# One inference step of a hybrid decoder layer: other PSUM bank counts, new states on two tags, and a group norm four quarter-units later

## The chip, the cores and the metric

The kernel runs on one core of one Trainium2 chip. The time is that of the whole program on the device, in microseconds (us). Before the change three runs took 1208.07, 1210.54 and 1215.57 us; their median is 1210.54 us.

## The reference

One layer of a decoder with two branches. There are 272 prompt rows (16 learned meta tokens and 256 prompt tokens) and 64 sample rows (8 sequences of 8 new tokens, which continue from carried states). All in float32.

```python
xn = rms_norm(h, norm_w)
proj = xn @ w_in                       # 2048 -> z_ssd, xBC, dt, z_pool, u, two gates
xbc_act, conv_new = causal_dwconv(xbc, conv_hist, conv_w, conv_b)      # 4 taps, silu
dt = softplus(dt_raw + dt_bias);  a = -exp(a_log)
y, state = ssd_segment(...)            # per chunk: y_diag + y_off, h = h * decay + B^T xdt
y = (y + xs * d_skip) * silu(z_ssd)
yg = y.reshape(..., 4, 512)            # gated norm over each of the 4 groups
yg = yg * rsqrt(mean(yg * yg) + EPS)
branch_ssd = (yg * ssd_norm_w) @ w_proj_ssd
mixed = einsum(pooled, pool_mix_w) + pool_mix_b    # pooled: causal means less u, per group
branch_pool = (mixed * pool_scale * silu(z_pool)) @ w_proj_pool
h_new = h + (gate_ssd * branch_ssd + gate_pool * branch_pool) @ w_out
y_out = rms_norm(h_new, final_norm_w)
```

The new states of the sample sequences (32 heads x 64 x 128 for each of 8) are outputs too.

## The kernel before

**Units and quarters.** The weights are cut into 156 units (UNITS, line 50), in this order: B 0 to 3, C 4 to 7, xs 8 to 23, z 24 to 39, then the SSD gate (gs) and the branch product (br), the pool stage (u, zp, mix), the pool gate (gp), its product (bp), and the output (wo, and wx at the end). A unit gives 128 output columns for all rows. Its 16 chunks of K are multiplied three times each (high weights with high operand, high with low, low with high; lines 235 to 237, half_k), 48 matmuls into one PSUM accumulator. A quarter-unit is 12 of them. Quarter q of unit i has the number 4i + q.

**Order.** Everything is laid out by hand (manual_schedule): each engine runs its instructions in the order in which the program issues them. The main loop (line 869) goes through the quarters. Before a quarter's matmuls it issues, for a half-unit three halves ahead, the high part of the weights on ACT (line 147, in even quarters), and after it the low part on DVE (line 153, in odd quarters); the load of a raw half on SP's queue (line 136) follows the low part that frees its buffer. After a quarter's matmuls tick(q) issues what was put down for that quarter with at(q, f) or later(d, f); later(1, f) is the next quarter's tick. A function that stands in a tick earlier than another was put down earlier.

**PSUM.** Eight banks go to three tags of the pool `ps`: "acc" for accumulators (NACC, line 32), "tr" for transposes, state-space outputs and some accumulators (NTR), and "st" (two, the pool's default) for sums, spreads, state products. A new tile of a tag takes the bank of an older one and its first writer waits for that one's last reader, on whichever engine it is.

**The state-space stage.** ssd_stages_of(g) puts the stages of group g down from tick 52 + 24g on (SSD_AT, SSD_STEP), so groups 0 to 3 begin at 52, 76, 100 and 124. The plan (line 622) holds offsets. Those that matter here: s_yoff1 at 8 and 10 (an "st" tile each, copied by ACT a tick later), s_dec(2) and s_dec(3) at 10 and 12 (differences on DVE, a tick later exponentials on ACT at lines 518 to 522, another later the products with cb on DVE at lines 528 and 530), s_y(2) and s_y(3) at 15 and 17 (line 560, "tr"; they read those products), s_new(q) at 17, 19, 21, 23, s_yoff2 at 20 and 21 (line 585, "tr"; read on DVE at lines 594 to 596), and s_pstate at 25 ("st"). s_new(q) is what gives pair q of the sample sequences its new state: two matmuls (line 613, "st") for sequences 2q and 2q + 1, each added to the decayed old state by DVE one tick later (line 615). The old states are decayed on POOL (line 605).

**The gated norm.** z_evac (line 639), one tick after a z unit, multiplies by rstd (line 637), a tick later takes silu on ACT (645), then multiplies into y on DVE (646), and three ticks after the evacuation squares on ACT: the first unit of a group into the tile gn[g] (line 649; tag "ss", one buffer), the others into a tile that POOL adds to gn[g] (line 654). norm_group(g) sits at tick 4 x (unit of z 4g + 3) + 9, that is 117, 133, 149 and 165. It calls spread_rstd (line 160): matmuls with gn[g] as the stationary operand into an "st" tile (line 165), one tick later scale and square root (lines 170 and 171), two later the reciprocal with a Newton step and three diagonal matrices on DVE (174 to 179), three later matmuls that spread the result over the partitions into another "st" tile (184), four later the products with y on DVE (661). y_split(g) (line 665) cuts y into a high and a low part for the br units and sits at ticks 170 to 173; br 0 is unit 44 (quarters 176 to 179, and its last quarter reads group 3).

Of the kernel before, what the change touches and what calls it, by code (L numbers as in the profile page):

```python
# [6 lines left out]
F32 = mybir.dt.float32  # L7
# [21 lines left out]
CBW = 480  # L29
CB2 = 400  # L30
NU0 = 8
NACC, NTR, NWARM = 3, 3, 16
SSD_AT, SSD_STEP = 52, 24
NWXS = 6
CHUNK = ((0, 128), (128, 128), (256, 64))
# [33 lines left out]
def hybrid_step(tc, ctx, io):  # L69
# [7 lines left out]
    ps = ctx.enter_context(tc.tile_pool(name="ps", bufs=2, space=PSUM))  # L77
# [6 lines left out]
    def slot(name, shape, dt=F32):  # L84
        tag = free_slots.pop(0)
        t = pool_of(tag).tile(shape, dt, tag=tag, name=name)
        live[name] = tag
        return t
# [6 lines left out]
    def drop(*names):  # L95
        for n in names:
            free_slots.append(live.pop(n))
# [14 lines left out]
    def pc(name, i):  # L112
        o, _ = _PC[name]
        return par[:, o + i:o + i + 1]
# [4 lines left out]
    def at(q, f):  # L119
        assert q >= now[0]  # L120
        sched.setdefault(q, []).append(f)

    def later(d, f):
        at(now[0] + d, f)
# [19 lines left out]
    def prep_hi(i, h):  # L144
        r = raws[i, h]
        hi = slot(f"wxh{i}_{h}", [128, HW], F32R) if kept(i, h) else wp.tile([128, HW], F32R, tag="hi", name=f"hi{i}_{h}")
        S.activation(hi, r, AF.Copy)  # L147
        whl[i, h] = hi
# [11 lines left out]
    def spread_rstd(ss, n, scale, name, done):  # L160

        at_ = (0, 128, n - 128)
        p = ps.tile([128, 512], F32, tag="st", name=f"ps_sum{name}")
        for i, t0 in enumerate(at_):
            PE.matmul(p[:, i:i + 1], lhsT=ss[:, t0:t0 + 128], rhs=ones[:, 0:1], start=True, stop=True, skip_group_check=True)
        v, t, r = (tp.tile([128, 3], F32, tag=f"f{j}", name=f"sr{name}{j}", bufs=1) for j in range(3))
        dg = tp.tile([128, 3, 128], F32, tag="dg", name=f"dg{name}", bufs=1)

        def f1():
            V.tensor_scalar(out=v, in0=p[:, 0:3], scalar1=scale, scalar2=EPS, op0=ALU.mult, op1=ALU.add)  # L170
            S.activation(t, v, AF.Sqrt)

        def f2():
            V.reciprocal(out=r, in_=t)
            V.tensor_tensor(out=t, in0=r, in1=r, op=ALU.mult)
            V.scalar_tensor_tensor(out=t, in0=t, scalar=-0.5, in1=v, op0=ALU.mult, op1=ALU.mult)
            V.scalar_tensor_tensor(out=r, in0=t, scalar=1.5, in1=r, op0=ALU.add, op1=ALU.mult)
            for i in range(3):
                V.tensor_scalar(out=dg[:, i, :], in0=ident, scalar1=r[:, i:i + 1], scalar2=None, op0=ALU.mult)

        def f3():
            q = ps.tile([128, 512], F32, tag="st", name=f"ps_rs{name}")
            for i, t0 in enumerate(at_):
                PE.matmul(q[:, t0:t0 + 128], lhsT=ones, rhs=dg[:, i, :], start=True, stop=True, skip_group_check=True)
            later(1, lambda: done(q))
        later(1, f1)
        later(2, f2)
        later(3, f3)
# [225 lines left out]
    def ssd_stages_of(g):  # L414
        sd = ssd["p"]
        Bg, Cg = Bs[:, g, :], Cs[:, g, :]
        st = {}
# [189 lines left out]
        def s_new(q):  # L607
            def f():
                for b in (2 * q, 2 * q + 1):
                    p = ps.tile([128, 512], F32, tag="st", name=f"ps_hn{g}_{b}")  # L610
                    j = b % 4
                    r = st["R"][32 * j:32 * j + 3 * DEC, b // 4, :].bitcast(F32R)
                    PE.matmul(p, lhsT=r[:, 512:XB], rhs=r[:, 0:512], start=True, stop=True, tile_position=(32 * j, 0))  # L613
                    h = st["hin", q][:, b % 2, :]
                    later(1, lambda h=h, p=p: V.tensor_tensor(out=h, in0=h, in1=p, op=ALU.add))
            return f
# [40 lines left out]
    def norm_group(g):  # L657
        def scale(r):
            for c in range(4):
                y = xs[g][:, c, NMETA:T]  # L660
                V.scalar_tensor_tensor(out=y, in0=y, scalar=pc("ssd_norm_w", 4 * g + c), in1=r[:, :TV], op0=ALU.mult,
                                       op1=ALU.mult)
        spread_rstd(gn[g], TV, 1.0 / 512, f"g{g}", scale)

    def y_split(g):
        h = slot(f"yh{g}", [128, 4, TV], F32R)
        l = slot(f"yl{g}", [128, 4, TV], F32R)
        y = xs[g][:, :, NMETA:T]
        S.activation(h, y, AF.Copy)
        yh.append(h)  # L670
        yl.append(l)

        def low():
            V.tensor_tensor(out=l, in0=y, in1=h.bitcast(F32), op=ALU.subtract)
            drop(f"xs{g}")
        later(1, low)
# [116 lines left out]
    def both_parts(q):  # L793
        for e, t in enumerate((mh, ml)):
            S.activation(fin["hl"][:, 4 * q:4 * q + 4, e, :], t[q][:, :, 256:TV].bitcast(F32), AF.Copy)
# [50 lines left out]
    first = {}  # L846
    for i, (kind, idx) in enumerate(UNITS):
        first.setdefault((kind, idx), i)
    for g in range(G):
        at(4 * first["z", 4 * g + 3] + 9, lambda g=g: norm_group(g))  # L850

    tscope = ExitStack()

    def late():
        scope.close()
        extra["p"] = ctx.enter_context(tc.tile_pool(name="slots2", bufs=1))
        free_slots.extend(f"x{j}" for j in range(10))
        extra["t"] = tscope.enter_context(tc.tile_pool(name="tp2", bufs=2))
        drop("Bs", "Cs")
        SY.dma_start(out=io["opold"], in_=io["spold"])  # L860
        for g in range(4):
            at(4 * first["gs", 0] + 10 + g, lambda g=g: y_split(g))

    prep(*halves[6])
# [4 lines left out]
    for i, (kind, idx) in enumerate(UNITS[:NU - 4]):  # L869
        if i < 2:  # L870
            at(14 + 2 * i, lambda i=i, k=kind, j=idx: evac(i, k, j, acc2[i]))
            continue
        if i == NU0:
            start.close()
            ssd["p"] = scope.enter_context(tc.tile_pool(name="ssd", bufs=1))
            for g in range(G):
                for d, f in ssd_stages_of(g):
                    at(SSD_AT + SSD_STEP * g + d, f)
        if (kind, idx) == ("gs", 0):
            late()  # L880
        if (kind, idx) == ("u", 0):
            drop(*[n for q in range(4) for n in (f"yh{q}", f"yl{q}")])
        if (kind, idx) == ("bp", 0):
            drop(*[n for q in range(4) for n in (f"xh{q}", f"xl{q}")])
        if (kind, idx) == ("wo", 0):
            drop(*[n for q in range(4) for n in (f"ph{q}", f"pl{q}")])
            for q in range(3):
                hn[q] = slot(f"hn{q}", [128, 4, TV])
                SY.dma_start(out=hn[q], in_=io["xT"][:, 4 * q:4 * q + 4, NMETA:T])
            tscope.close()  # L890
            extra["f"] = ctx.enter_context(tc.tile_pool(name="fin", bufs=1))
            fin["xy"] = extra["f"].tile([128, 2, 512], F32, name="xres")
            fin["xw"] = slot("xrw", [128, 2, 512])
            fin["hl"] = extra["f"].tile([128, KT, 2, 64], F32R, name="hl")
            SY.dma_start(out=fin["xy"], in_=io["xres"][0:256, :].rearrange("(c p) f -> p c f", c=2))
            SY.dma_start(out=fin["xw"][0:64, 0, :], in_=io["xres"][256:320, :])
            SY.dma_start(out=fin["xw"][:, 1, :], in_=io["fwb"])
            for q in range(4):
                at(4 * i + 2 + 4 * q, lambda q=q: both_parts(q))
        if kind == "mix":  # L900
            acc = [ps.tile([128, 512], F32, tag="tr" if c < 3 else "acc", name=f"acc{i}_{c}", bufs=3) for c in range(4)]
        else:
            acc = ps.tile([128, 512], F32, tag="tr" if i == 3 else "acc", name=f"acc{i}", bufs=NACC)
        for qq in range(4):
            if qq % 2 == 0:
                n = place.get(2 * i + qq // 2 + 3, len(halves) - 1)
                for x in halves[done:n + 1]:
                    prep_hi(*x)
            else:
                for x in halves[done:n + 1]:  # L910
                    prep_lo(*x)
                done = n + 1
                load_to(n + 5)
            quarter_mm(i, qq, acc, kind, idx)
            if kind == "mix":
                at(4 * i + qq + 1, lambda g=idx, c=qq, a=acc: mix_evac(g, c, a[c]))
            elif qq == 3:
                at(max(4 * i + 4, 14 + 2 * i), lambda i=i, k=kind, j=idx, a=acc: evac(i, k, j, a))
            tick(4 * i + qq)
# [56 lines left out]
    for j, (t0, n) in enumerate(CHUNK):  # L976
        acc = ps.tile([128, 512], F32, tag="acc", name=f"accx{j}", bufs=NACC)
# [115 lines left out]
```

## Time and profile before

| | |
|---|---|
| median of three runs | 1210.54 us |
| profiled execution, its own time | 1208.65 us |
| its span, first to last instruction | 1206.7 us |
| mean granted TensorE clock | 0.998 |
| PE, PEld busy | 1191.6, 1152.8 us |
| DVE, ACT, POOL busy | 731.7, 531.9, 84.1 us |

PE is TensorE's matmuls and PEld its weight loads, DVE is VectorE, ACT ScalarE, POOL GpSimd, and SP the queue that issues transfers. A row of the timeline gives the start in us from the span's start, the length in us, the engine, the line, the operation, output<-input by the program's names, the shapes, how many instructions are merged in it, and in brackets how long the engine stood idle before it and what ended that. In a merged row matmuls overlap, and a matmul's length has its way through the array in it, so the next one starts earlier than the row ends. A row of the windows gives the stretch, its length, then for PE, PEld, DVE, ACT and POOL the busy time and the number of instructions, the granted clock as a share of full speed, the mean busy share of the transfer engines and GB/s.

### The profile page before, as it was taken

The numbers are of one execution on the slowest core, as the hardware profiler recorded it, in microseconds if no ns is written. First come the engines' busy times: TensorE is split into PE (matmuls) and PEld (weight loads), VectorE is DVE, ScalarE is ACT, GpSimd is POOL, SyncE is SP. The second block draws the span as 40 slices with busy tenths as digits, with TensorE's granted clock in tenths as the row PEclk, the third lists the DMA queues.
The fourth block names the chain that finished last, engine by engine and source line by source line (L and its number), as shares of the span: only waits on it lengthen the run. The fifth ranks groups of instructions, "written<-read, shape, count | busy, mean of one in ns | idle before, by whom it ended". The sixth has DMA issues, their size and how long they took to land.

```text
span 1206.7 us, 19815 instructions
## 1 busy us (share of the span) xinstructions
PE 1191.6 (99%) x8015; PEld 1152.8 (96%) x8015; DVE 731.7 (61%) x1138; ACT 531.9 (44%) x728; POOL 84.1 (7%) x82
## 2 busy tenths in 40 slices
PE   9999999999999999999999999999999999999996
PEld 7999889898989999999999999999999999999995
DVE  7786898898875644444457474765454455555634
ACT  6555636383835433333333433434343333335531
POOL 0000141433231000000000000000000000000000
PEclk9999999999999999999999999999999999999999
DMA  7645667676764444444456454544444444446612
GB/s 282 198 150 168 215 214 241 215 256 215 228 209 156 148 149 155 142 157 144 154 162 179 152 158 159 157 153 156 145 152 154 144 156 147 151 176 230 227 40 88
DMA packets 86087, 207.66 MB, mean 172 GB/s; under 512 B 26876, under 2 KB 32092, under 8 KB 85980
## 3 DMA queue, kind: packets, MB, share of 16 engines
q1 hardware_dynamic: 85836, 205.36, 51.4%
q8 instruction: 63, 1.03, 0.4%
q0 software_dynamic: 160, 1.03, 0.3%
q14 instruction: 28, 0.23, 0.1%
HBM read 189.05 MB, written 17.77 MB: 171 GB/s over the span
## 4 chain that ended last, share of the span: by engine, by line
PE 92%; DVE 4%; DMA 2%; issue 1%; ACT 1%; SPq 0%; DVEq 0%; ACTq 0%
PE acc L235 28%; PE acc L236 28%; PE acc L237 28%; PE accx L985 2%; DVE cacc L342 1%; PE acc L280 1%; DVE lo L153 1%; DMA bc<-acT 1%; PE ps_y L560 1%; PE ps_st L545 1%; PE ps_hn L613 1%; DMA raw<-wall 0%; DVE M L513 0%; DVE M L528 0%; PE ps_yo L572 0%
## 5 line engine op out<-in xcount | busy, mean ns | idle before, releaser
L147 ACT ACTIVATE hi<-raw 128x1024 fp32r<-128x1024 f32 x306 | 323.8, 1059 | 548.4 <-PE acc L236 387.9
L153 DVE TENSOR_TENSOR lo<-raw,hi 128x1024 fp32r<-128x1024 f32 x306 | 380.2, 1243 | 246.6 <-ACT hi L147 246.5
L235 PE MATMUL acc<-xh,hi 128*128 128x320 f32 (+4 forms) x1632 | 511.8, 314 | 0.0
L236 PE MATMUL acc<-xl,hi 128*128 128x320 f32 (+4 forms) x1632 | 507.7, 311 | 0.0
L237 PE MATMUL acc<-xh,lo 128*128 128x320 f32 (+4 forms) x1632 | 506.7, 310 | 0.0
L235 PEld LDWEIGHTS acc<-xh,hi 128*128 128x128 f32 x1632 | 306.6, 188 | 6.3 <-issue 4.0
L237 PEld LDWEIGHTS acc<-xh,lo 128*128 128x128 f32 x1632 | 306.9, 188 | 0.0
L236 PEld LDWEIGHTS acc<-xl,hi 128*128 128x128 f32 x1632 | 306.7, 188 | 0.0
L236 PE MATMUL acc<-yl,hi 128*128 128x320 f32 x256 | 79.0, 309 | 0.0
L235 PE MATMUL acc<-yh,hi 128*128 128x320 f32 x256 | 79.0, 308 | 0.0
L237 PE MATMUL acc<-yh,lo 128*128 128x320 f32 x256 | 78.9, 308 | 0.0
L237 PE MATMUL acc<-ph,lo 128*128 128x320 f32 x256 | 78.9, 308 | 0.0
L236 PE MATMUL acc<-pl,hi 128*128 128x320 f32 x256 | 78.8, 308 | 0.0
L235 PE MATMUL acc<-ph,hi 128*128 128x320 f32 x256 | 78.7, 308 | 0.0
L237 PE MATMUL acc<-mh,lo 128*128 128x320 f32 x192 | 59.3, 309 | 0.0
L235 PE MATMUL acc<-mh,hi 128*128 128x320 f32 x192 | 59.3, 309 | 0.0
L236 PE MATMUL acc<-ml,hi 128*128 128x320 f32 x192 | 59.3, 309 | 0.0
L605 POOL TENSOR_TENSOR hin<-hin,E 128x512 f32<-128x512 f32 x32 | 49.5, 1575 | 49.2 <-ACT E L522 32.9
L342 DVE SCALAR_TENSOR_TENSOR cacc<-rawf,par,cacc 128x360 f32<-128x360 f32 (+1 forms) x72 | 50.7, 705 | 1.8
L237 PEld LDWEIGHTS acc<-ph,lo 128*128 128x128 f32 x256 | 48.1, 188 | 0.0
L236 PEld LDWEIGHTS acc<-pl,hi 128*128 128x128 f32 x256 | 48.1, 188 | 0.0
L235 PEld LDWEIGHTS acc<-ph,hi 128*128 128x128 f32 x256 | 48.0, 188 | 0.0
(237 smaller groups left out, 1194.3 us busy)
## 6 DMA issues: line engine op xcount, KB each, us to landing
raw<-wall SPq DMA_DIRECT2D x312, 512.0 KB
hin<-ssmT SPq DMA_DIRECT2D x16, 512.0 KB
ossms<-hin SPq DMA_DIRECT2D x16, 512.0 KB
bc<-acT SPq DMA_DIRECT2D x8, 672.0 KB
x<-xT SPq DMA_DIRECT2D x3, 672.0 KB
R<-tail SPq DMA_DIRECT2D x32, 60.0 KB
hn<-xT SPq DMA_DIRECT2D x3, 640.0 KB
opool<-u SPq DMA_DIRECT2D x16, 100.0 KB
```

The costliest lines, as they stand in the source:

```text
L147: S.activation(hi, r, AF.Copy)
L153: V.tensor_tensor(out=lo, in0=r, in1=hi.bitcast(F32), op=ALU.subtract)
L235: PE.matmul(acc[:, :n], lhsT=hi[:, c], rhs=bh, start=first, stop=False)
L236: PE.matmul(acc[:, :n], lhsT=hi[:, c], rhs=bl, start=False, stop=False)
L237: PE.matmul(acc[:, :n], lhsT=lo[:, c], rhs=bh, start=False, stop=last)
L280: PE.matmul(acc2[u][:, :T], lhsT=w[part // 2][:, cc], rhs=(wl if part == 1 else wh)[q][:, c, :], start=(k == 0 and part == 0), stop=(k == ...
L342: V.scalar_tensor_tensor(out=a[:, a0:], in0=r[:, a0 + k:k + ACCW], scalar=pc("conv_w", 4 * c + k), in1=a[:, a0:], op0=ALU.mult, op1=ALU.add)
L545: PE.matmul(p, lhsT=st["bt"][:, i, :], rhs=st["xdt"][:, i, :], start=(i == 0), stop=False)
L560: PE.matmul(p[64 * e:64 * e + 64, a:b], lhsT=st["xdt"][:n, i, 64 * hh:64 * hh + 64], rhs=m[:n, e, o:o + b - a], start=(i == 0), stop=(i == ...
L605: GP.tensor_tensor(out=hv, in0=hv, in1=E, op=ALU.mult)
L613: PE.matmul(p, lhsT=r[:, 512:XB], rhs=r[:, 0:512], start=True, stop=True, tile_position=(32 * j, 0))
L985: PE.matmul(acc, lhsT=st, rhs=wx(part, k), start=(k == 0 and o == 0), stop=(k == KT - 1 and part == 1))
```

## The change

"acc" goes from three banks to two and "tr" from three to four ("st" keeps two). Unit 2 joins unit 3 in "tr", and the four accumulators of a mix unit all take "tr". Of the new states, pairs 0 and 2 stay in "st" and pairs 1 and 3 go to "tr". norm_group goes from +9 to +13, to ticks 121, 137, 153 and 169. The last y_split no longer has a tick of its own but follows one tick after the products of its group's norm, at 174 and not 173.

```diff
-NACC, NTR, NWARM = 3, 3, 16
+NACC, NTR, NWARM = 2, 4, 16
...
         def s_new(q):
             def f():
                 for b in (2 * q, 2 * q + 1):
-                    p = ps.tile([128, 512], F32, tag="st", name=f"ps_hn{g}_{b}")
+                    p = ps.tile([128, 512], F32, tag=("st", "tr")[q % 2], name=f"ps_hn{g}_{b}", bufs=(2, NTR)[q % 2])
...
                 V.scalar_tensor_tensor(out=y, in0=y, scalar=pc("ssd_norm_w", 4 * g + c), in1=r[:, :TV], op0=ALU.mult,
                                        op1=ALU.mult)
+            if g == 3:
+                later(1, lambda: y_split(g))
         spread_rstd(gn[g], TV, 1.0 / 512, f"g{g}", scale)
...
     for g in range(G):
-        at(4 * first["z", 4 * g + 3] + 9, lambda g=g: norm_group(g))
+        at(4 * first["z", 4 * g + 3] + 13, lambda g=g: norm_group(g))
...
         SY.dma_start(out=io["opold"], in_=io["spold"])
-        for g in range(4):
+        for g in range(3):
             at(4 * first["gs", 0] + 10 + g, lambda g=g: y_split(g))
...
         if kind == "mix":
-            acc = [ps.tile([128, 512], F32, tag="tr" if c < 3 else "acc", name=f"acc{i}_{c}", bufs=3) for c in range(4)]
+            acc = [ps.tile([128, 512], F32, tag="tr", name=f"acc{i}_{c}", bufs=NTR) for c in range(4)]
         else:
-            acc = ps.tile([128, 512], F32, tag="tr" if i == 3 else "acc", name=f"acc{i}", bufs=NACC)
+            acc = ps.tile([128, 512], F32, tag="tr" if i in (2, 3) else "acc", name=f"acc{i}",
+                          bufs=NTR if i in (2, 3) else NACC)
```

## The prediction

> **What bounds the kernel now.** I read the page first.
>
> ```profile
> span 1206.7 us, 19815 instructions
> PE 1191.6 (99%) x8015; PEld 1152.8 (96%) x8015; DVE 731.7 (61%) x1138; ACT 531.9 (44%) x728; POOL 84.1 (7%) x82
> ```
>
> PE is busy for 99% of the span, so time can only be won or lost where PE stands still. Next, the busy time by stretches, a steady one and one in the state-space stage:
>
> ```profile
> 450.00:600.00 150.00, 150.00 (x1026) 150.00 (x1025) 63.04 (x64) 48.66 (x52) 0.00 (x0) 1.00 0.44 151
> 150.00:170.00 20.00, 18.40 (x124) 16.22 (x121) 19.66 (x29) 7.93 (x15) 14.38 (x13) 1.00 0.61 187
> ```
>
> In the steady stretch 1026 matmuls take 150 us, 146.2 ns each, so a quarter-unit (12 matmuls) is 1.755 us, which I call a quarter. In the second stretch PE loses 1.6 us while DVE is full (19.66 of 20). PE's timeline shows where: at the matmuls for the new states, line 613. The rows below hold a wait in state-space group 0, one in group 1, the undisturbed form, and (two rows) one in group 2.
>
> ```profile
> 161.52 1.09 PE L613 MATMUL ps_hn<-R 24*128 24x512 f32 x2 [1.50 <-DVE hin L615]
> 221.54 1.09 PE L613 MATMUL ps_hn<-R 24*128 24x512 f32 x2 [0.24 <-DVE hin L615]
> 279.54 0.50 PE L613 MATMUL ps_hn<-R 24*128 24x512 f32 x2
> 285.52 0.50 PE L613 MATMUL ps_hn<-R 24*128 24x512 f32 x1
> 287.02 0.46 PE L613 MATMUL ps_hn<-R 24*128 24x512 f32 x1 [1.00 <-PE ps_hn L613]
> ```
>
> Undisturbed, a pair runs side by side in 0.50. At 161.52 it waits 1.50 for the additions that free its banks and then runs one after the other (1.09 - 0.50 = 0.59): 2.09. At 221.54: 0.24 + 0.59 = 0.83. At 285.52 the second of the pair comes 1.46 late. That one's releaser is on DVE:
>
> ```profile
> 285.00 1.92 DVE L661 SCALAR_TENSOR_TENSOR xs<-xs,par,ps_rsg 128x320 f32<-128x320 f32 x4
> ```
>
> It ends at 286.92, and PE goes on 0.10 later. The bank was held by the spread rstd of norm group 0, which these four products read. So a matmul can wait for a reader that stands later in the program. In all 2.09 + 0.83 + 1.46 = 4.38 us.
>
> **The change, part by part.** *New states alternating.* Pairs 1 and 3 move to the four-bank tag, so in "st" a pair follows the one before after four quarters, not two. The additions then have two quarters more (3.5 us) than a wait of at most 2.09 needs. The waits of groups 0 and 1 go. In "tr" a bank comes round four tiles later, and every reader of such a tile is planned at least two quarters ahead of the next writer. Gain 2.09 + 0.83, and 1.46 because norm group 0's spread now comes at quarter 124, behind pair 2 of state-space group 2. If DVE were later than two quarters, the waits would return: zero is the other bound.
>
> *Two accumulators.* Unit u+2 now needs u's evacuation. Units 2 and 3 go to "tr", so the tightest place is unit 6 on unit 4's bank:
>
> ```profile
> 57.27 0.21 DVE L332 TENSOR_TENSOR rawf<-acc,rstd_x 128x64 f32<-128x64 f32 x1
> 57.91 0.31 PE L235 MATMUL acc<-xh,hi 128*128 128x324 f32 x1
> ```
>
> Unit 4's last read ends at 57.48 and unit 6 starts at 57.91: 0.43 us to spare. Later evacuations have about a unit (four quarters, 7.0 us) less DVE's lateness. Cost zero; if the cover is gone, PE waits the excess. The same answer goes for the mix units (four banks of one tag, free for eight units before), and for the last split, which still has three quarters (5.3 us) before its operand is multiplied.
>
> *Norm four quarters later.* This adds a wait. The sum of squares lives in tile "ss", which has one buffer. The next group's first square (line 649) writes it in tick 119, 135 and 151; the matmul that reads it (line 165) moves from tick 117, 133 and 149 to 121, 137 and 153. It used to read first; now the square stands two quarters ahead of the read and must wait for PE. Before, PE read it here, and ACT wrote later:
>
> ```profile
> 273.78 0.72 PE L165 MATMUL ps_sumg<-ones,ss 128*128 128x1 f32 x6
> 276.36 0.46 ACT L649 ACTIVATE ss<-xs 128x320 f32<-128x320 f32 x1
> 279.55 1.06 ACT L147 ACTIVATE hi<-raw 128x1024 fp32r<-128x1024 f32 x1 [2.74 <-issue]
> 281.89 1.28 ACT L645 ACT_TABLE_LOAD   x1 [1.28 <-DVE sz L637]
> 283.18 0.47 ACT L645 ACTIVATE sz<-sz 128x320 f32<-128x320 f32 x1
> ```
>
> ACT runs in order, so behind the held square stand the next weight split, silu, and at group 1 the decay exponentials. On DVE the low weight halves, silu products and rstd chain wait for those. The weights themselves are safe (prepared six quarters, 10.5 us, ahead; so are the loads on SP, which follow the low halves). PE meets the delay at what reads the norm:
>
> ```profile
> 274.54 0.16 DVE L170 TENSOR_SCALAR srg<-ps_sumg 128x3 f32<-128x3 f32 x1 [1.02 <-PE ps_sumg L165]
> 284.05 0.58 DVE L594 TENSOR_TENSOR yof<-ps_yt,E 64x128 f32<-64x128 f32 x2
> 284.67 0.29 DVE L596 TENSOR_TENSOR xs<-xs,yof 128x128 f32<-128x128 f32 x1
> 286.84 0.48 DVE L646 TENSOR_TENSOR xs<-xs,sz 128x320 f32<-128x320 f32 x1
> 285.00 0.60 PE L585 MATMUL ps_yt<-ident,yo 128*128 128x128 f32 x4
> 332.49 1.22 DVE L153 TENSOR_TENSOR lo<-raw,hi 128x1024 fp32r<-128x1024 f32 x1
> ```
>
> *Norm group 0*, from the sum's end at quarter 121. "st" has two banks, and the sum with both halves of pair 2 wants three: the second half waits for line 170. ACT: square 0.46, split 1.06 (1.52), table 1.28, silu 0.47 (3.27). DVE: low half 1.22 (2.74), lines 594 and 596 0.87 (3.61), line 646 0.48 (4.09), line 170 0.16 (4.25), handover 0.10: 4.35. PE is there after the transposes, 0.50. Stall 3.85.
>
> *Norm group 1* (137) has the longest queue on ACT, without a gap before:
>
> ```profile
> 319.39 0.20 ACT L171 ACTIVATE srg<-srg 128x3 f32<-128x3 f32 x1 [0.72 <-DVE srg L170]
> 319.50 0.45 ACT L649 ACTIVATE ss<-xs 128x320 f32<-128x320 f32 x1
> 322.62 0.32 ACT L519 ACTIVATE M<-M 80x160 f32<-80x160 f32 x1
> 326.90 1.05 ACT L147 ACTIVATE hi<-raw 128x1024 fp32r<-128x1024 f32 x1
> 320.41 0.17 DVE L174 RECIPROCAL srg<-srg 128x3 f32<-128x3 f32 x1
> 321.20 0.68 DVE L179 TENSOR_SCALAR dgg<-ident,srg 128x128 f32<-128x128 f32 x3
> 323.53 0.98 DVE L528 TENSOR_TENSOR M<-M,cb 128x800 f32<-128x800 f32 x1
> 324.43 0.31 DVE L530 TENSOR_TENSOR M<-M,cb 80x160 f32<-80x160 f32 x1
> 331.63 0.48 DVE L637 TENSOR_TENSOR sz<-acc,rstd_x 128x320 f32<-128x320 f32 x1
> 330.34 1.04 PE L560 MATMUL ps_y<-M,xdt 128*64 128x256 f32 x12
> ```
>
> From the sum's end: the exponentials end at 322.94 - 319.50 = 3.44, their products (324.74 - 323.53 = 1.21) at 4.65. PE wants them for line 560 after two quarters, 3.6: stall 1.15 with the handover. Then line 560 (0.97 of it before the next matmul) and a quarter bring PE to the spread at 7.5. ACT reaches the end of the split at 327.95 - 319.50 = 8.45; table 1.28 and root 0.20 make 9.93. The chain to the diagonals takes 321.88 - 320.41 = 1.47 with POOL idle, and twice that beside POOL:
>
> ```profile
> 278.50 0.16 DVE L174 RECIPROCAL srg<-srg 128x3 f32<-128x3 f32 x1
> 280.73 0.68 DVE L179 TENSOR_SCALAR dgg<-ident,srg 128x128 f32<-128x128 f32 x3
> 277.45 3.03 POOL L540 TENSOR_TENSOR xdt<-xdt,dend 128x512 f32<-128x512 f32 x2
> 325.27 7.37 POOL L605 TENSOR_TENSOR hin<-hin,E 128x512 f32<-128x512 f32 x4 [12.17 <-ACT E L522]
> ```
>
> 281.41 - 278.50 = 2.91. POOL will run here (its decays follow these exponentials); only some of DVE's operations met it, so I take the middle, 2.2: 12.2 with the handover, stall 4.7 (4.0 to 5.4). Pair 0 of state-space group 3 (141), in the spread's bank and on PE behind a quarter and 0.97, waits for the four products (1.92), ahead of which DVE has lines 637, 563 and 153 (331.63 to 333.71, 2.08): 12.1 + 2.08 + 1.92 = 16.1 against 12.2 + 0.69 + 1.755 + 0.97 = 15.6. Stall 0.6. In sum 1.15 + 4.7 + 0.6 = 6.45.
>
> *Norm group 2* (153): square, split, silu, split, table, root: 0.46 + 1.06 + 0.47 + 1.05 + 1.28 + 0.20 = 4.5, chain 1.47, handover: 6.1, against three quarters, 5.3. Stall 0.85.
>
> New stalls 3.85 + 6.45 + 0.85 = 11.15, less 4.38: **+6.8**. The profiled execution took 1208.65 (span 1206.7), so 1215.4; it lies 1.9 below the median of the runs, 1210.54. I write 1216.
>
> A price to weigh: after the row of 281.89 silu starts at 283.18, nothing beyond 1.28 is seen. The Trainium skill (ScalarE: Activation LUTs, What ACT_TABLE_LOAD costs) adds a drain of about 1.38; by that norm group 1, with three loads in its chain, would cost an estimated 4.1 more and the time be 1220. By the row it is 1216, and the trace disagrees with the page.
>
> **The rivals.** *The hold costs nothing* (0.18). If ACT came to the square two quarters late anyway, or the buffer were not the same, only the banks would count: -4.38, and one new collision, because group 1's spread at 140 meets pair 0 at 141. There 286.92 - 282.46 = 4.46 passed from spread to products' end,
>
> ```profile
> 282.46 0.94 PE L184 MATMUL ps_rsg<-dgg,ones 128*128 128x128 f32 x6
> ```
>
> against 0.69 + 1.755 + 0.97 = 3.4: +1.1. Time 1208.65 - 3.3 = 1205.4. Against it: at 319.50 ACT wrote before quarter 135 had ended on PE, so it is early.
>
> *The clock drops* (0.15). Stalls of about 4 us may let the granted clock fall. At the end of the trace PE's last accumulation ended near 1196.9 and the next matmul came at 1201.1:
>
> ```profile
> 1196.90:1202.20 5.30, 0.47 (x3) 0.29 (x2) 3.42 (x11) 1.52 (x4) 0.00 (x0) 1.00 0.38 148
> 1202.20:1206.70 4.50, 0.00 (x0) 0.00 (x0) 0.67 (x3) 0.00 (x0) 0.00 (x0) 0.50 0.38 117
> ```
>
> Full for 5.3 us, then half for at least 4.5. That much after a stall costs 2.25 us: 1217.7 for one, 1220 for two. Waits up to 1.5 left it at 1.00. The Trainium skill (TensorE: Matmul & The Clock Gate, What's actually happening) lets one idle window of about 3.4 us halve it, with the window running free, so a stall of 3.9 would seldom hold a whole one.
>
> *DVE sets the pace* (0.06): in the full stretch above, the removed waits return as others; only the new stalls count: 1208.65 + 11.15 = 1219.8.
>
> *Two accumulators bind* (0.04): DVE held behind ACT evacuates more than a unit late in groups 1 to 3. From 7.0 us of lateness on, PE waits what exceeds it; a chain of 12.2 in group 1 and about 9 elsewhere would give 5 + 2 + 2 = 9 on top: 1224.
>
> **How the numbers follow.** The sum as worked has 0.57; its own range is 1211.5 to 1218.5. The range 1204.5 to 1220 takes in the first rival and most of the next two. About 1% (12.1 us) is what a measurement tells from no change: 1198.4 and 1222.6. Slower than that: the accumulators 0.04, and 0.06 from the clock on top of the long ends of group 1. Faster: 0.02, since 4.38 is all there is. Within: 0.88.
>
> **What would show it.** Pairs at line 613 in groups 0 and 1 run in 0.50 with no wait. ACT's square, line 649, ends just behind line 165, three times, with ACT idle up to two quarters ahead of it. PE waits at line 613 near group 0's sum, at 560, 184 and 613 near group 1's, briefly at 184 near group 2's. It would be wrong if line 649 ran ahead of line 165, if weights (line 237) came late, or if accumulations waited for DVE.

## The result, and the profile after

The changed kernel takes 1222.64 us (median of six runs, 1222.17 to 1223.6); the kernel before, run beside it on the same chip, 1208.07. The ratio is 1.0118 (95% interval 1.01 to 1.0136), 14.6 us slower. The forecast was 1216 within 1204.5 to 1220, so the time lies above the range, and the slowdown passes the 1% (12.1 us) that the forecast gave as the limit of no change.

The page of the changed kernel's profiled execution, whose own time is 1223.6 us; the third row is the granted clock in forty slices of 30.5 us:

```profile
span 1221.9 us, 19928 instructions
PE 1197.7 (98%) x8015; PEld 1158.0 (95%) x8015; DVE 733.5 (60%) x1138; ACT 532.6 (44%) x729; POOL 80.1 (7%) x82
PEclk9999999998989999999999999999999999999999
```

The span is 15.2 us longer. PE does the same 8015 matmuls and is busy only 6.1 us longer (1197.7 against 1191.6), so some 9 us are new idle time and most of the rest is matmuls that ran slower: two slices, those from 275 and from 336 us, show a granted clock below 9 tenths, where before showed none. To place it, PE's waits of the changed kernel (engine, tile and line, what it waited for; us in total, times, the longest):

```profile
PE ps_rsg L184 <- DVE dgg L179: 8.3, 4, 7.1
PE ps_r L966 <- DVE small L960: 4.2, 1, 4.2
PE ps_hn L613 <- DVE srg L170: 3.3, 1, 3.3
PE ps_y L560 <- DVE M L528: 0.7, 1, 0.7
```

The 4.2 at line 966 stands at the end of the program and was there before. The other three rows are new, and all name what the forecast named: the spread of the norm (184), the second half of pair 2 (613), the product that needs the decays (560). Behind each stands ACT. Its timeline:

```profile
281.44 0.47 ACT L649 ACTIVATE ss<-xs 128x320 f32<-128x320 f32 x1 [9.33 <-PE ps_sumg L165]
328.30 0.47 ACT L649 ACTIVATE ss<-xs 128x320 f32<-128x320 f32 x1 [8.85 <-PE ps_sumg L165]
377.70 0.47 ACT L649 ACTIVATE ss<-xs 128x320 f32<-128x320 f32 x1 [7.25 <-PE ps_sumg L165]
```

Three times the next group's first square stands at the head of ACT's queue, with ACT idle for 7 to 9 us, until line 165 has read the old content of "ss". What PE made of it, on its timeline:

```profile
160.16 0.50 PE L613 MATMUL ps_hn<-R 24*128 24x512 f32 x2
219.29 0.50 PE L613 MATMUL ps_hn<-R 24*128 24x512 f32 x2
281.78 0.49 PE L613 MATMUL ps_hn<-R 24*128 24x512 f32 x1
285.59 0.79 PE L613 MATMUL ps_hn<-R 24*128 24x512 f32 x1 [3.32 <-DVE srg L170]
342.62 0.76 PE L184 MATMUL ps_rsg<-dgg,ones 128*128 128x128 f32 x2 [7.12 <-DVE dgg L179]
343.55 0.79 PE L184 MATMUL ps_rsg<-dgg,ones 128*128 128x128 f32 x2 [0.16 <-DVE dgg L179]
344.56 0.80 PE L184 MATMUL ps_rsg<-dgg,ones 128*128 128x128 f32 x2 [0.22 <-DVE dgg L179]
```

The first two rows are the pairs that waited before, now undisturbed. Then come the two large stalls, 3.32 at norm group 0 and 7.5 (7.12 + 0.16 + 0.22) at norm group 1. And a single matmul of line 613 takes 0.79 where 0.49 was enough just before: the clock. The windows of the changed kernel (stretch, length, busy time and instructions of PE, PEld, DVE, ACT and POOL, then the granted clock, transfer share and GB/s), each large stall and what comes behind it:

```profile
281.78:285.30 3.52, 0.49 (x2) 0.18 (x1) 2.36 (x5) 3.50 (x5) 0.00 (x0) 0.97 0.07 8
285.30:292.10 6.80, 6.51 (x23) 6.07 (x24) 4.65 (x15) 0.73 (x3) 0.87 (x1) 0.52 0.79 227
335.30:339.90 4.60, 0.20 (x2) 0.00 (x0) 4.53 (x7) 4.13 (x6) 4.60 (x4) 0.97 0.40 123
339.90:350.10 10.20, 7.09 (x30) 5.77 (x30) 8.79 (x13) 3.17 (x4) 5.93 (x7) 0.51 0.29 99
```

While PE stands still, ACT is full in the first stall (3.50 of 3.52) and DVE in the second (4.53 of 4.60). The second stall goes on into the last row: the clock fell at 339.9, and PE went on at 342.62. Then PE runs at half clock: 6.51 and 7.09 us of its busy time at 0.52 and 0.51, which, if a matmul takes twice as long at half clock, would have been 3.4 and 3.6. Counted so, 3.1 + 3.5 = 6.6 us are lost to the clock; the run with filler below shows that this is an upper count.

The account then closes to half a us. Against before, this profile has the 4.38 of removed waits, new waits of 3.3 at line 613, 0.7 at line 560 and 8.3 at line 184 (7.5, and 0.8 for norm group 2) = 12.3, and 6.6 of clock: +14.5. The two profiled executions differ by 1223.6 - 1208.65 = 14.95.

### The profile page after: what moved, and what is told of

It is laid out like the page before. It is cut to its first block, busy times and chain, and to the rows that moved or that the text cites. A ratio compares the mean times of both kernels' runs of the same rounds, so it can differ in the third digit from the quotient of the medians.

```text
span 1221.9 us, 19928 instructions
## 1 busy us (share of the span) xinstructions
PE 1197.7 (98%) x8015; PEld 1158.0 (95%) x8015; DVE 733.5 (60%) x1138; ACT 532.6 (44%) x729; POOL 80.1 (7%) x82
## 3 DMA queue, kind: packets, MB, share of 16 engines
q8 instruction: 63, 1.03, 0.4%
q0 software_dynamic: 160, 1.03, 0.3%
## 4 chain that ended last, share of the span: by engine, by line
PE 96%; DVE 2%; ACT 1%; DMA 0%; issue 0%; SPq 0%; DVEq 0%; ACTq 0%
PE acc L235 29%; PE acc L236 29%; PE acc L237 29%; PE accx L988 2%; PE ps_y L560 1%; PE acc L280 1%; PE ps_yo L572 1%; PE ps_hn L613 1%; PE ps_st L545 1%; DVE lo L153 0%; DMA raw<-wall 0%; PE ps_xt L470 0%; PE ps_cb L436 0%; ACT hi L147 0%; PE ps_rsg L184 0%
```

## The experiments

The theory: ACT's queue, held by the square of line 649 behind the moved read of line 165, makes the whole slowdown, and the bank counts none. Rivals: two accumulators bind; the banks make a loss of their own; the clock and not the wait is what costs. Every run was timed beside the kernel before on its own chip, whose medians were 1207.49 us (first four), 1207.98 (next three) and 1207.91 (the rest). Differences below are to that median, so the changed kernel stands at +14.6.

**The norm alone, banks as before.**

```diff
-        at(4 * first["z", 4 * g + 3] + 9, lambda g=g: norm_group(g))
+        at(4 * first["z", 4 * g + 3] + 13, lambda g=g: norm_group(g))
```

with the last split one tick behind its products, and nothing else of the change.

> Only the later norm (with its last split), all banks and tags as before. If the hold of ACT behind the matmul of line 165 is the cause, the whole loss is here, and the waits of the new states in state-space groups 0 and 1 (about 3 us) stay on top of it: 14.6 + 3, so about 1225 us, with ACT idle 7 to 9 us ahead of line 649 three times. If the banks are the cause (two accumulators, new states among the transposes), this is within 2 us of the kernel before.

Measured 1226.25 us, ratio 1.0147 (1.0119 to 1.0176). Its profile has the three rows of PE's waits at lines 184, 613 and 560 as the changed kernel has them, to the tenth (8.3, 3.3, 0.7).

The move of the norm makes the whole loss by itself. Its four runs lie between 1221.53 and 1227.82, wider than any other variant's here; the profile is of the lowest. The others have a lower mean clock (0.990 and 0.991 against 0.992), but where they lost more was not seen.

**The banks alone**: the changed kernel with `+ 9` and the last split's own tick put back.

> All banks and tags as in the change, the norm and the last split at their old ticks. Hold theory: the waits of state-space groups 0 and 1 go (2.2 + 0.9), the one of 1.5 at 285 us stays because the spread still lies ahead of pair 2: about 3 us under the kernel before, 1205 us. Banks theory: as slow as the change, 1222 us, with waits for evacuations.

Measured 1207.2 us, ratio 0.999 (0.9978 to 1.0002). The banks cost nothing, and they bring hardly anything: -0.3 us, where the forecast had counted 2.92 for them. No pair of groups 0 and 1 waits in its profile, so the waits did go. The two further profiles of the kernel before, below, show why that is worth so little. The wait at pair 2 that only the norm's place makes is still there:

```profile
283.84 0.46 PE L613 MATMUL ps_hn<-R 24*128 24x512 f32 x1 [1.28 <-issue]
```

**A second buffer for the sum of squares**, in the changed kernel; the same for the pool stage's tile of that tag.

```diff
-            gn[g] = tp.tile([128, TV], F32, tag="ss", name=f"ss{g}", bufs=1)
+            gn[g] = tp.tile([128, TV], F32, tag="ss", name=f"ss{g}", bufs=2)
```

> The change with two buffers for the tile ss, so that the next group's first square needs no read to be over; the norm is as late as in the change. Hold theory: the holds, the stalls behind them and both drops of the clock go; left are the gain of 4.4 and one new wait of about 1 us where the spread of norm group 1 meets pair 0: 1205 us. If lateness itself costs (the chain meets the new states and POOL's decays, whatever ACT waits for), it stays at 1215 to 1222.

Measured 1208.01 us, ratio 0.9998 (0.9984 to 1.0011). One word, `bufs=2`, takes 14 of the 14.6 us back, and the holds with their two large stalls are gone. Its profile shows two reasons why it isn't 1205. The norm at `+ 13` has a price of its own, hold or not: the spread of norm group 1 at 140 runs into the state-space stage, with 1.6 us of waits at line 184 and 0.25 at pair 0 behind it, and from the first matmul of quarter 139 to that of quarter 142 this profile takes 11.7 us, that of the next run 8.6. And in the profiled execution, the slowest of this kernel's runs, two accumulators did bind once, where the forecast saw 0.43 us to spare, and the clock fell behind it (PE's timeline, then the window):

```profile
59.85 0.38 PE L235 MATMUL acc<-xh,hi 128*128 128x324 f32 x1 [1.84 <-DVE rawf L332]
```

```profile
60.40:63.80 3.40, 3.40 (x14) 3.40 (x14) 3.25 (x5) 2.21 (x5) 0.00 (x0) 0.51 0.06 20
```

**Two buffers and the norm a quarter earlier** (`+ 12`).

> As the run with two buffers, with the norm three quarters late, not four: the spread of norm group 1 then comes at quarter 139 and is read a quarter ahead of pair 0. Hold theory: no wait at line 613 is left, 4.4 us under the kernel before, 1203.7 us, and within 1.5 us of the run with two buffers. If lateness itself costs, between the kernel before and the change.

Measured 1203.98 us, ratio 0.9967 (0.9951 to 0.9982): faster than both kernels, by 3.5 us against before. The 1203.7 of the hold theory came out; that the run with four quarters would lie within 1.5 us of it did not. It lies 4.0 above, so the fourth quarter costs about that much even without the hold. Its longest waits:

```profile
PE ps_r L966 <- DVE small L960: 4.2, 1, 4.2
PE ps_warm L230 <- DVE ones L227: 1.1, 1, 1.1
PE acc L280 <- ACT hi L147: 0.9, 1, 0.9
PE acc L280 <- ACT xh L247: 0.6, 1, 0.6
```

Nothing of the state-space stage or the norm is left among them: the three at 230 and 280 belong to the start, the first to the end.

**The same with the banks of before**: three accumulators, three "tr", the last split at its own tick, and only the alternating pairs, two buffers and `+ 12`. It asks the rival of two accumulators.

> Two buffers for ss and the norm three quarters late, as in the fastest run so far (1204.0), but with three banks for the accumulators and three for tr as before the change; the new states still alternate, and the last split keeps its own tick. If two accumulators cost nothing, the same 1204 us. If unit 6 sometimes waits for unit 4's bank (0.43 us to spare in the trace of before, 1.8 us waited in one profile), up to 2 us less on average and no wait of line 235 for line 332. If hn in three tr banks meets the transposes, 1 to 3 us more.

Measured 1204.2 us, ratio 0.9971 (0.9959 to 0.9983), the same as with two accumulators. In the median the third one is worth nothing, although its absence showed once, in the row at 59.85.

**Filler for the stalls.** In the changed kernel, 14 matmuls of constants stand ahead of the first half of pair 2 of group 2, in its bank, and 28 ahead of the spread of norm group 1, in its bank; the real ones overwrite them. PE works while it waits, and the wait itself stays.

```diff
+    def filler(t, n):
+        for _ in range(n):
+            PE.matmul(t[:, 0:128], lhsT=ones, rhs=ones, start=True, stop=True, skip_group_check=True)
...
             q = ps.tile([128, 512], F32, tag="st", name=f"ps_rs{name}")
+            if name == "g1":
+                filler(q, 28)
...
+                    if (g, b) == (2, 4):
+                        filler(p, 14)
                     j = b % 4
```

> The change, with PE kept busy in its two long waits: 14 matmuls of 128 columns on constants (about 0.22 us each, 3.1 us) ahead of the first of pair 2 in state-space group 2, and 28 (6.2 us) ahead of the spread of norm group 1; their results are overwritten by the real matmuls. Both waits stay as long as they are. If the slow matmuls behind the two waits come from the clock that fell because PE stood still, the granted clock stays at 1.00 and about 2.8 and 3.2 us come back: 1217 us. If they come from anything else, 1222.6 us stays.

Measured 1220.85 us, ratio 1.0109 (1.0089 to 1.013): +12.9, so 1.7 back, where 5.6 was expected. Its windows over the two sites:

```profile
283.80:287.70 3.90, 3.71 (x31) 3.28 (x29) 2.62 (x7) 3.78 (x6) 0.00 (x0) 1.00 0.16 26
287.70:294.10 6.40, 6.39 (x39) 5.72 (x40) 6.18 (x17) 2.79 (x4) 0.88 (x1) 1.00 0.73 224
334.70:344.20 9.50, 7.67 (x65) 7.10 (x63) 9.36 (x13) 4.06 (x6) 9.50 (x9) 1.00 0.31 107
344.70:348.10 3.40, 3.40 (x14) 2.71 (x15) 3.40 (x7) 2.38 (x3) 0.09 (x1) 0.50 0.36 116
```

With filler the clock stays at 1.00 through both stalls, and at these two sites it falls only once, for 3.4 us, behind the second one, whose filler had run out (7.67 busy of 9.50). From the first matmul of quarter 120 to that of quarter 156 this profile takes 100.8 us, the changed kernel's 104.5: 3.7 us came back with the waits still there. So the clock is a cost of its own, on top of the wait.

With the 1.7 us at most of the spell that is left, the clock is worth 5.4, not the 6.6 counted above. The rest is most likely the chain's: in the 6.6 are 2.35 us of the spread's own matmuls, which start about 1.0 us apart at half clock (342.62, 343.55, 344.56) and at full clock too (341.88, 342.90, 343.91 here), because each pair waits for its diagonal.

The median moved by less than 3.7. In this profile quarter 8 begins at 29.53 us, not at 27.25, and the cause lies ahead of any filler: the clock was at half there as well, behind two waits at the start of the program (PE's timeline, where line 286 is line 280 of the changed kernel, then the window):

```profile
8.53 0.89 PE L286 MATMUL acc<-xh,hi 128*128 128x336 f32 x2 [0.63 <-ACT xh L253]
10.25 1.49 PE L286 MATMUL acc<-xh,hi 128*128 128x336 f32 x4 [0.83 <-ACT hi L147]
```

```profile
10.20:13.60 3.40, 3.35 (x12) 3.35 (x13) 3.37 (x7) 2.36 (x4) 0.00 (x0) 0.50 1.02 420
```

Of the four runs the profiled one and one more have a mean clock of 0.995 and took 1222.1 and 1223.0; the other two have 0.997 and took 1219.2 and 1219.6. That these two had no such start is likely, but they have no profile.

**Group 3's decays left out.** The changed kernel without POOL's eight multiplications of the old states in state-space group 3, so that those new states lack the decay. It asks how much of norm group 1's 7.1 us POOL makes.

> The change without the decays of the old states in state-space group 3 (8 operations on POOL; those new states then lack the decay). ACT's hold is untouched. If the rstd chain of norm group 1 is stretched by POOL's use of what DVE shares with it, the chain of lines 174 to 179 falls from 6.0 us to about 1.5, PE's wait at line 184 from 7.3 to about 3, and that is short enough for the clock to stay up there: 1214 to 1216 us. If the hold alone makes the wait, 1222.6 us stays.

Measured 1219.03 us, ratio 1.0095 (1.0079 to 1.0111): +11.1, 3.5 less than the changed kernel, where 6.6 to 8.6 less was expected. Here are DVE's rows of norm group 1's chain, first in the changed kernel, where POOL is busy all the while, then without the decays:

```profile
338.55 0.16 DVE L174 RECIPROCAL srg<-srg 128x3 f32<-128x3 f32 x1
338.75 0.82 DVE L175 TENSOR_TENSOR srg<-srg 128x3 f32<-128x3 f32 x1
339.60 0.98 DVE L176 SCALAR_TENSOR_TENSOR srg<-srg,srg 128x3 f32<-128x3 f32 x1
340.62 0.78 DVE L177 SCALAR_TENSOR_TENSOR srg<-srg,srg 128x3 f32<-128x3 f32 x1
341.43 3.08 DVE L179 TENSOR_SCALAR dgg<-ident,srg 128x128 f32<-128x128 f32 x3
```

```profile
337.03 0.17 DVE L174 RECIPROCAL srg<-srg 128x3 f32<-128x3 f32 x1 [0.29 <-ACT srg L171]
337.24 0.16 DVE L175 TENSOR_TENSOR srg<-srg 128x3 f32<-128x3 f32 x1
337.44 0.16 DVE L176 SCALAR_TENSOR_TENSOR srg<-srg,srg 128x3 f32<-128x3 f32 x1
337.63 0.74 DVE L177 SCALAR_TENSOR_TENSOR srg<-srg,srg 128x3 f32<-128x3 f32 x1
338.41 0.68 DVE L179 TENSOR_SCALAR dgg<-ident,srg 128x128 f32<-128x128 f32 x3
```

344.51 - 338.55 = 5.96 against 339.09 - 337.03 = 2.06. (One POOL addition is left, from 337.49 to 338.35; the row at 337.63, which meets it, still takes 0.74.) And PE's wait for the chain falls from 7.12 to

```profile
338.84 1.41 PE L184 MATMUL ps_rsg<-dgg,ones 128*128 128x128 f32 x5 [4.49 <-DVE dgg L179]
```

About 3 had been expected, with the clock staying up. It still falls behind both stalls, for 3.4 and for 6.8 us; the second is

```profile
337.80:344.60 6.80, 5.76 (x24) 5.08 (x26) 5.48 (x12) 3.38 (x5) 0.55 (x1) 0.50 0.45 152
```

What covers the chain in the changed kernel is on POOL's timeline there:

```profile
333.98 6.58 POOL L605 TENSOR_TENSOR hin<-hin,E 128x512 f32<-128x512 f32 x4 [18.81 <-ACT E L522]
341.34 4.10 POOL L605 TENSOR_TENSOR hin<-hin,E 128x512 f32<-128x512 f32 x4
```

The decays wait for ACT's exponentials, which the held square delays; but it delays the chain as well, and it isn't what brings the two together. In the run with two buffers, which has no hold, the chain of norm group 1 takes 334.10 - 328.11 = 5.99 us, beside the same decays:

```profile
331.02 3.08 DVE L179 TENSOR_SCALAR dgg<-ident,srg 128x128 f32<-128x128 f32 x3
323.54 6.59 POOL L605 TENSOR_TENSOR hin<-hin,E 128x512 f32<-128x512 f32 x4 [11.51 <-ACT E L522]
```

With the norm at `+ 12` the chain runs ahead of the decays, in 1.48 us with two buffers. So POOL's part in the loss comes from the fourth quarter, and the hold adds its own delay to it.

**The kernel before, looked at twice more.** They ask whether the waits of groups 0 and 1 are the same in every execution.

> The kernel before, unchanged, for another profile. The banks alone gained about 1 us where the profile of before promised 3. If the waits of state-space groups 0 and 1 differ from one execution to the next (DVE later or earlier by when the broadcast of the decays lands), this profile shows other waits at line 613 than 1.5 and 0.24 us, down to none, and the one of 1.0 us at group 2 unchanged. If they are fixed, the same three waits.

> The kernel before once more, unchanged: as the run ahead of it.

Measured 1207.21 and 1210.52 us. In the forecast's profile the pair of group 0 waited 1.50, and its second half then came 0.59 behind the first. In the first of these two it didn't wait, but its second half came 0.60 behind (the row merges the two); in the second it waited 1.83, and the clock fell behind it:

```profile
159.85 1.09 PE L613 MATMUL ps_hn<-R 24*128 24x512 f32 x2
```

```profile
162.39 1.10 PE L613 MATMUL ps_hn<-R 24*128 24x512 f32 x2 [1.83 <-DVE hin L615]
```

```profile
164.10:167.50 3.40, 3.40 (x15) 3.34 (x14) 3.04 (x7) 0.69 (x1) 1.17 (x3) 0.51 0.62 137
```

The delay goes with a transfer. DVE, whose additions the pair waits for, has earlier in the group the differences of line 513, which wait for a broadcast; in the first of these two and in the second that row is

```profile
137.20 1.36 DVE L513 TENSOR_SCALAR M<-bc,acum 128x256 f32<-128x256 f32 x6 [2.20 <-DMA bc<-acT]
```

```profile
139.73 0.99 DVE L513 TENSOR_SCALAR M<-bc,acum 128x256 f32<-128x256 f32 x4 [4.05 <-DMA bc<-acT]
```

(The second view ends behind four of the six.) In the forecast's profile it started at 138.86, and in the run with the norm alone, which keeps the old pairs, at 136.69; there the pair's second half came 0.17 behind:

```profile
159.78 0.66 PE L613 MATMUL ps_hn<-R 24*128 24x512 f32 x2
```

In order of that start, 136.69, 137.20, 138.86, 139.73, the second half is late by 0.17, 0.60, 2.09 and 2.43 (the wait and its distance behind the first): little where the broadcast was early, much where it was late. No run moved the broadcast alone, so that it is the cause is argued and not shown. At group 1 the second half was late by 0.83 in the forecast's profile and by 0.52 and 0.09 in these two. Group 2's wait, which a read of DVE made, was 1.00, 1.00 and 1.01 in the three profiles of before.

**One buffer and `+ 12`**: the changed kernel with the norm a quarter earlier.

> The change with the norm three quarters late, and with the one buffer for ss: against the fastest run (1204.0 us) only the buffer differs. Hold theory: the read stands one quarter behind the square, not two, but the chain that PE waits for still begins at the read's end, so most of the loss is there: 1216 to 1222 us, with the clock falling again. If the hold counts by its own length, half the loss is left: 1213 us. If the buffer doesn't matter at this offset, 1204 us.

Measured 1211.98 us, ratio 1.0034 (1.0021 to 1.0046): +4.1. That is below the 1216 to 1222 of the hold theory and nearest to the 1213 expected if half the loss is left. ACT is still held, at the same place:

```profile
279.04 0.47 ACT L649 ACTIVATE ss<-xs 128x320 f32<-128x320 f32 x1 [7.14 <-PE ps_sumg L165]
319.98 0.47 ACT L649 ACTIVATE ss<-xs 128x320 f32<-128x320 f32 x1 [7.09 <-PE ps_sumg L165]
```

But the read is a quarter sooner. Pair 2 of group 2 doesn't wait, and the chain of norm group 1 runs ahead of POOL's decays (1.48 us), so that line 184 waits 1.24 and not 7.12. The longest wait is now at pair 0 of state-space group 3, whose bank the products of norm group 1 read until 336.49:

```profile
336.60 0.47 PE L613 MATMUL ps_hn<-R 24*128 24x512 f32 x1 [3.30 <-issue]
```

Behind it the clock falls once, for 3.4 us. At `+ 12` the one buffer costs 4.1 + 3.5 = 7.6 us, at `+ 13` 14.6 - 0.5 = 14.1. A quarter, 1.755 us on PE, makes 6.5 us of difference, so the loss doesn't follow the length of the hold. Almost all of it is the stall at pair 2 with the half clock behind it, which only `+ 13` has: from quarter 120 to 125 the changed kernel takes 6.6 us longer than with two buffers, and this run 0.2 longer than the run with two buffers and `+ 12`.

## Why the prediction was off

Term by term, as the forecast put it and as the profile of the changed kernel has it (us):

| term | forecast | measured |
|---|---|---|
| removed waits, groups 0, 1 and pair 2 | -4.38 | -4.38 against that one profile; -0.3 in the median for the banks alone |
| norm group 0, pair 2 at line 613 | 3.85 | 3.3 (3.8 late, counted as the 1.46 was) |
| norm group 1, line 560 | 1.15 | 0.7 |
| norm group 1, spread at line 184 | 4.7 (4.0 to 5.4) | 7.5 |
| norm group 1, pair 0 | 0.6 | 0 |
| norm group 2, line 184 | 0.85 | 0.8 |
| granted clock | 0 in the sum, 2.25 a stall as a rival | 3.1 and 3.5 as counted; 5.4 at most by the run with filler |
| sum | +6.8 | +14.5 |

**The mechanism was right.** The square held behind the moved read, three times, and PE's waits at 613, 560 and 184 are what the forecast described; the run with the norm alone and the one with two buffers show that they are the cause. Four of the stalls came within 0.6 us of their working. ACT stood longer ahead of the square, 7 to 9 us where up to two quarters (3.5 us) had been forecast, but what counts for PE starts at the sum's end. Pair 0 at 141 didn't wait: the products that free its bank ended at 348.35, and PE, at half clock, came there at 350.13. At full clock it would have come at about 347.7 (345.01 + 1.755 + 0.97), an estimate, and 0.6 too early, as forecast.

**The step that failed most is the clock** (of the 8 us missing, 6.6 as counted and at most 5.4 by the run with filler). The forecast set it beside the sum, as another way it could go with a chance of 0.15, and priced it on 2.25 for each stall; 0.06 went to the clock on top of the long ends of group 1, beyond 1222.6, which is nearest to what came. The clock goes with the sum: in every profile here it fell behind a stall of over 3 us that had no filler in it, so whoever believes in 11 us of stalls has to add it. Even the forecast's own price would have given 1215.4 + 4.5 = 1219.9. In the profile of the changed kernel it was more, because full clock didn't come back before 6.8 and 10.2 us. That length isn't fixed: behind the same first stall, 3.32, it came back after 3.4 us in the profiles of the norm alone and of the run without decays.

The reason given for the small chance was that waits up to 1.5 had left the clock at 1.00. That is a bound from below only, and nothing in the trace of before bounded it at 3.9. The Trainium skill was cited there for a whole idle window of about 3.4 us (TensorE: Matmul & The Clock Gate, What's actually happening). The runs don't bear this out as a limit: the clock fell behind waits of 1.83 and 1.84 us too, and behind 0.63 and 0.83 together at the start of the run with filler.

**The second is the size of one term**, norm group 1's chain: 2.2 us, with 2.91 called the long end, and 5.96 in the profile. The 2.91 came from a stretch in which POOL met some of DVE's operations; here it met all of them. The forecast had written that POOL's decays follow the exponentials that the hold delays, and didn't go on to place them: 6.58 + 4.10 us of POOL's work, from 4.6 us ahead of the chain to its end. With two buffers the chain at the same place took 5.99, so this follows from the place of the norm and not from the hold. Without the decays the wait is 4.49, against 4.7 forecast.

**The third is the gain.** 4.38 was read from one execution. Of it the 1.46 at pair 2 is steady. The 2.92 of groups 0 and 1 go with the time at which a broadcast lands: in the three other profiles with the old pairs they were 0.17, 1.12 and 2.52, the last with a drop of the clock on top. This is hidden in the account above, since the profile of before that it starts from had the longest waits of the four; in the medians the banks alone bring 0.3.

**The rivals.** The rival that the hold costs nothing fell with the first timeline of ACT. That DVE takes the removed waits back fell too, but its price had a true part: the removed waits were worth less than they looked. That two accumulators bind was seen once, for 1.84 us, and not in the medians (1203.98 with two, 1204.2 with three). The price that the forecast weighed from the Trainium skill (ScalarE: Activation LUTs, What ACT_TABLE_LOAD costs), 4.1 us more at norm group 1, would have made the wait at line 184 8.8; without POOL on the chain it was 4.49.

## What to carry to other kernels

Before a read is moved later, look for the next writer of what it reads: with one buffer, that writer now waits for the read, and with it everything that stands behind it in its engine's order; here a second buffer took 14 of the 14.6 us back, and with the norm a quarter earlier the change became a gain of 3.5. When a sum of waits is forecast and one of them is over 3 us long on PE, add the half-clock matmuls behind it, and ask what the chain meets in its new place. Before counting a removed wait as gain, see in a second execution whether it is there again.

## What the runs showed of the hardware

Ahead of the last wait of the program, the half clock came in spells of 3.4, 6.8 and 10.2 us, always multiples of 3.4, so the shortest drop cost up to 1.7 us of matmul time. In the rows from 286.74 on in the changed kernel the matmuls start 0.267 us apart at half clock, where full clock gives 0.146. It came behind stalls of 3.3 to 7.5 us, but also behind waits of 1.83 us at a pair (the third profile of the kernel before) and 1.84 at an accumulator, and behind 0.63 and 0.83 within 2.4 us at the start of the run with filler; not behind the 1.50 of the forecast's profile. No single length of a wait is the limit in these runs.

Beside POOL's multiplications, short DVE operations take several times as long: a 128x3 multiplication 0.82 in place of 0.16, a 128x128 scaling 1.03 (3.08 for three) where three took 0.68 end to end without POOL's decays. The Trainium skill (SBUF — State Buffer, Who interferes with whom) has DVE's second pair of ports shared with GpSimd under an exclusive lock; the rows agree in kind; of the chain's seven operations six were slowed.
